# First feed-forward column of a transformer layer: copy, weight halves, sums and the scaling of the last rows emitted in another order

## The chip, the cores and the metric

The kernel runs on one core of one Trainium2 chip. The metric is the device time of one execution in microseconds, as the median of several runs. The engines are named as in the profile: PE (matmul), DVE (vector), ACT (scalar), POOL (GpSimd) and SP, which issues most of the transfers. Each engine works through its own queue in order, and waits on semaphores for the others.

## The reference

One layer of an encoder runs over two sequences of 1024 tokens with model width 1024: attention with low-rank queries and keys, and a Fourier mixing beside it, then a gated feed-forward block, all in float32. The part that matters here is the end of the layer:

```python
    x = x + ga1 * mix
    h2 = rmsnorm(x, g_ffn) * (1.0 + sc2) + sh2
    ffn = (jax.nn.silu(h2 @ w_gate) * (h2 @ w_up)) @ w_down
    return x + ga2 * ffn
```

`w_gate` and `w_up` are 1024 x 2816; the kernel cuts the 2816 into 22 columns of 128.

## The kernel before

**Precision.** A float32 product is made from two halves of each operand: a high half rounded by ACT (L62, a cast) and a low half, the difference, by DVE (L63). `split` and `hl` make them. One product of 128 x 128 x 512 takes three matmuls (L78, L79, L80).

**Seven products instead of eight.** Gate and up weights of a column are a 2 x 2 block matrix, as are the activations (two halves of the width, two halves of the tokens). Four subtractions (`sums_w`) turn a column's four weight blocks into seven operands; the activations have seven as well, `H[0]` to `H[6]`, each with a high tile and a low tile (`H40`, `H41` for operand 4). A column is seven steps in the order of operands 0, 5, 1, 6, 4, 3, 2, and a step is 12 matmuls into one of three PSUM banks x, y, z: x in steps one and three, y in steps two, four and six, z in steps five and seven. Between them ACT copies x (L1358), applies silu (L1367, L1378), and DVE adds banks to values in SBUF (L138) and multiplies (L1379, L1382). A step that goes on in a bank must wait until the sum of that bank has been read.

**Where the stretch lies.** The output projection of the last 256 rows of sequence 1 (`out_proj`, tile `gb`) runs into the first column of sequence 0 (`n` = 0, here column one). At that time four things are unfinished:

- the operands `H[4]`, `H[3]`, `H[2]` of sequence 0, which the generator `prep` loads and splits;
- the weights of column one, of which `sums_w` has made the operands in `w0`; the first two are split before the column (tiles `fw`), the other five inside it (tiles `wh`, `wl`);
- the weights of column two, loaded by SP into four `val` tiles (L1244), summed on DVE (L135) and split;
- the last two blocks of 128 rows (`norm3`). Block `u` = 1 lies in the upper half of tile `X1`. POOL stores these rows to memory (L1149), ACT takes the sum of squares (L1153), POOL makes the reciprocal root (L103 to L110, tile `rs_r`), and DVE scales the rows in place (L1155). In column two `flip2` transposes them (L1162) and ACT and SP write them out as activations of sequence 1.

Besides, POOL makes sums of the down weights (`down_combos`, tile `tdb`, loaded at L1266, stored to `t_d`) and of the weights from column three on (tile `rgu`, loaded at L1248). `rgu` of column three lies in tile `X0`, which first holds `w0`, then the loaded operand 2.

**What sets the order.** A scheduler orders each engine's queue at build time, from the order in which the code emits the instructions. `tc.issue_after(i)` places the instructions emitted under it behind instruction `i`; `behind()` does so for the last high and low half; `first(early, late)` puts one before another.

Of the kernel before, what the change touches and what calls it, by code (L numbers as in the profile page):

```python
# [16 lines left out]
ALU = mybir.AluOpType  # L17
# [35 lines left out]
def hybrid_encoder_kernel(ctx: ExitStack, tc: tile.TileContext, a: dict):  # L53
    nc = tc.nc

    here = {}
# [1017 lines left out]
    with ExitStack() as st:  # L1074
# [72 lines left out]
        def norm3(u, jk=None):  # L1147
            x2 = S.pop(("x2", 1, 3, u))
            nc.gpsimd.dma_start(x2_d[1][(6 + u) * P : (7 + u) * P, :], x2)  # L1149
# [5 lines left out]
            nc.vector.tensor_scalar(out=S["xn", 1, 3, u], in0=x2, scalar1=r[:, 0:1], scalar2=None, op0=ALU.mult)  # L1155

        def flip2(b, xn, bankf, hts):
            for g in range(4):
# [79 lines left out]
        for s in range(2):  # L1238
# [70 lines left out]
            if s == 0:  # L1309
                wts = [(fw[0][:, i, :], fw[1][:, i, :]) for i in range(2)]  # L1310
                fw = None
                next(prep, None)
                wts += [hl(w0[i]) for i in (2, 3)]
            else:
                wts = first_w
            A = {}
            late = None
            for n, f in enumerate(order):
                cur, nxt = wts, []
                src = combos(n + 1, s == 0 and n == 0) if n + 1 < NF else None  # L1320
                if late is not None:
                    put_s(*late)
                    late = None
                elif s == 0 and n > 0:
                    down_combos(n // 2)
                    if n % 4 == 1 and n < 20:
                        comb_h(1, n // 4 - 1) if n >= 5 else None

                def step(j, ps, k, first, src=src):
                    prod(ps, k, cur[j], first)  # L1330
                    if s == 0 and n == 0:
                        if j == 0:
                            cur.extend(hl(v) for v in w0[4:])
                            w0.clear()
                            norm3(1, S.pop("jk3").bitcast(BF16))
                        if j < 3:
                            with behind():
                                for _ in range(2):
                                    next(prep, None)
                            return  # L1340
                        if j == 3:
                            src = S["w1"] = sums_w(src, lambda i: val(), nc.vector)
                        src = S["w1"]
                        for i in ((), (), (), (0, 1), (2, 3), (4,), (5, 6))[j]:
                            nxt.append(hl(src[i]))
                    elif src is not None:
                        with ExitStack() as after:
                            if j == 1:
                                after.enter_context(tc.issue_after(here["p1"]))
                            nxt.append(hl(src[j]))  # L1350
                    if s == 0 and n == 1 and j == 2:
                        S.pop("w1", None)
                        flip2(3, [S.pop(("xn", 1, 3, u)) for u in range(2)], bank, lambda g: val())

                x, y, z = bank(), bank(), bank()
                step(0, x, 0, True)
                p1 = val()
                here["p1"] = nc.scalar.copy(p1, x).ins  # L1358
                step(1, y, 5, True)
                u2 = val()  # L1360
                here["u"] = add(u2, y, p1, nc.vector)
                if pending:
                    with tc.issue_after(here["u"]):
                        pending.pop(0)()
                step(2, x, 1, False)
                sg = val()
                nc.scalar.activation(sg, x, AF.Silu)  # L1367
                step(3, y, 6, False)
                u3 = val()
                here["u"] = add(u3, y, p1, nc.vector)  # L1370
                if pending:
                    with tc.issue_after(here["u"]):
                        pending.pop(0)()
                step(4, z, 4, True)
                add(u3, z, u3, nc.vector)
                step(5, y, 3, False)
                add(p1, y, p1, nc.vector)
                nc.scalar.activation(p1, p1, AF.Silu)  # L1378
                nc.vector.tensor_tensor(out=u3, in0=p1, in1=u3, op=ALU.mult)  # L1379
                step(6, z, 2, False)  # L1380
                add(u2, z, u2, nc.vector)
                nc.vector.tensor_tensor(out=u2, in0=sg, in1=u2, op=ALU.mult)  # L1382
                A[0, n % 2] = u2
# [294 lines left out]
```

## Time and profile before

| | |
|---|---|
| median of 3 runs | 2070.72 us (2069.9 to 2070.88) |
| profiled execution, its own time | 2073.43 us |
| its span, first to last instruction | 2071.7 us |
| PE busy | 2001.2 us, 97% |
| DVE, ACT, POOL busy | 1417.9, 902.8, 831.7 us |
| granted TensorE clock, mean | 0.991 |

In a timeline row stand start, duration, engine, line, operation, the tile written and the tiles read, the shape, and in brackets how long the engine had stood idle before it and what ended that. A matmul's duration overlaps the next one's: the distance of starts is what one costs. In a row of the waits stand the total in us, the times and the longest; in a row of the table by stretches the window, its length, the busy time and count of PE, the weight loads, DVE, ACT and POOL, then the granted clock, the share of the transfer engines and their GB/s.

### The profile page before, as it was taken

To read this page: it belongs to the slowest core of one execution; us is meant where nothing else is said; L and a number is where in the kernel's file an instruction comes from. 1 tells how busy PE (TensorE), PEld (TensorE's weight loads), DVE (VectorE), ACT (ScalarE), POOL (GpSimd) and SP (SyncE) were. 2 spreads that over 40 slices of the span, in tenths; PEclk is the share of its full clock that TensorE was granted. 3 is DMA by queue.
4 is the path that set the end of the run, shared out by engine and by line. 5 is a ranking of instruction groups with operands and counts; after the bars stand their busy time and mean duration, and the time that the engine had idled before them with its cause. 6 is when DMAs were issued, how large, how long until landed. Compare 5 with 4: busy or idle time off the path is not lost.

```text
span 2071.7 us, 28756 instructions
## 1 busy us (share of the span) xinstructions
PE 2001.2 (97%) x10044; PEld 1661.8 (80%) x10044; DVE 1417.9 (68%) x2097; ACT 902.8 (44%) x1765; POOL 831.7 (40%) x1026
## 2 busy tenths in 40 slices
PE   5899999999999997999999999999999999999997
PEld 2788877888888886888888888877788888888876
DVE  2757757766776777887777677777765566567684
ACT  2665534555565564333333356454333333336441
POOL 1455203111312313798788710223554454420142
PEclk8999999999999999999999999999999999999999
DMA  9586775544643465555555578675332232258662
GB/s 367 192 250 207 229 262 191 133 94 90 158 119 116 153 219 178 173 197 189 188 192 178 177 257 271 220 240 178 128 127 101 78 127 102 80 186 278 225 229 91
DMA packets 182942, 371.30 MB, mean 179 GB/s; under 512 B 19020, under 2 KB 58316, under 8 KB 179724
## 3 DMA queue, kind: packets, MB, share of 16 engines
q1 hardware_dynamic: 163660, 309.80, 45.0%
q0 software_dynamic: 19136, 59.65, 9.6%
q8 instruction: 79, 1.29, 0.3%
q14 instruction: 67, 0.55, 0.1%
HBM read 257.38 MB, written 120.39 MB: 182 GB/s over the span
## 4 chain that ended last, share of the span: by engine, by line
PE 52%; DVE 4%; DMA 2%; issue 1%; POOL 1%; ACT 1%; SPq 0%; DVEq 0%; ACTq 0%; POOLq 0%
PE bank L79 18%; PE bank L78 18%; PE bank L80 17%; DVE wl L63 2%; DVE val L138 1%; DMA val<-x_d 1%; DMA draw<-s_d 1%; POOL val L138 1%; DMA draw<-t_d 1%; ACT wh L62 0%; DVE val L1485 0%; POOL rs_y L106 0%; DMA draw<-in_w_down_dram 0%; DVE val L1459 0%; SPq L1444 0%
## 5 line engine op out<-in xcount | busy, mean ns | idle before, releaser
L79 PE MATMUL bank<-H,wh 128*128 128x512 f32 x1224 | 477.4, 390 | 9.3 <-DVE H L63 9.3
L78 PE MATMUL bank<-H,wh 128*128 128x512 f32 x1224 | 477.9, 390 | 5.5 <-DVE val L138 4.1
L80 PE MATMUL bank<-H,wl 128*128 128x512 f32 x1224 | 476.8, 390 | 0.0
L138 DVE TENSOR_TENSOR val<-bank,val 128x512 f32<-128x512 f32 x244 | 166.7, 688 | 166.8 <-PE bank L80 162.6
L79 PEld LDWEIGHTS bank<-H,wh 128*128 128x128 f32 x1224 | 230.3, 188 | 57.2 <-DVE H L63 9.6
L78 PEld LDWEIGHTS bank<-H,wh 128*128 128x128 f32 x1224 | 230.3, 188 | 56.2 <-DVE val L138 6.8
L80 PEld LDWEIGHTS bank<-H,wl 128*128 128x128 f32 x1224 | 230.2, 188 | 48.3
L63 DVE TENSOR_TENSOR wl<-draw,wh 128x512 fp32r<-128x512 f32 x286 | 201.0, 737 | 88.5 <-ACT wh L62 87.2
L62 ACT CAST wh<-draw 128x512 fp32r<-128x512 f32 x286 | 168.6, 620 | 157.3 <-PE bank L79 80.6
L79 PE MATMUL bank<-wl,wh 128*128 128x512 f32 x572 | 223.8, 391 | 2.5 <-DVE wl L63 2.4
L138 POOL TENSOR_TENSOR val<-val 128x512 f32<-128x512 f32 x58 | 83.3, 1444 | 351.0 <-DVE val L1459 186.4
L78 PE MATMUL bank<-wh 128*128 128x512 f32 x572 | 222.7, 389 | 0.0
L80 PE MATMUL bank<-wh,wl 128*128 128x512 f32 x572 | 222.7, 389 | 0.0
L62 ACT CAST wh<-rgu 128x512 fp32r<-128x512 f32 x171 | 106.3, 622 | 248.8 <-PE bank L79 192.8
L63 DVE TENSOR_TENSOR wl<-val,wh 128x512 fp32r<-128x512 f32 x133 | 143.3, 1079 | 74.0 <-ACT wh L62 73.9
L63 DVE TENSOR_TENSOR wl<-rgu,wh 128x512 fp32r<-128x512 f32 x171 | 163.8, 958 | 2.5 <-ACT wh L62 2.4
L62 ACT CAST wh<-val 128x512 fp32r<-128x512 f32 x133 | 82.3, 622 | 183.9 <-PE bank L79 162.5
L135 POOL TENSOR_TENSOR val<-rgu 128x512 f32<-128x512 f32 x80 | 112.6, 1407 | 103.6 <-DMA rgu<-in_wgu_dram 99.9
L79 PEld LDWEIGHTS bank<-wl,wh 128*128 128x128 f32 x572 | 107.3, 188 | 28.9 <-DVE wl L63 6.7
L78 PEld LDWEIGHTS bank<-wh 128*128 128x128 f32 x572 | 107.4, 188 | 22.8 <-ACT wh L62 0.4
L80 PEld LDWEIGHTS bank<-wh,wl 128*128 128x128 f32 x572 | 107.4, 188 | 21.9
L945 DVE TENSOR_REDUCE mx<-ps_s 128x1 f32<-128x1024 f32 x64 | 78.2, 1222 | 60.9 <-PE ps_s L940 60.5
(374 smaller groups left out, 4125.2 us busy)
## 6 DMA issues: line engine op xcount, KB each, us to landing
rgu<-in_wgu_dram SPq DMA_DIRECT2D x86, 512.0 KB
draw<-s_d SPq DMA_DIRECT2D x143, 256.0 KB
s_d<-val POOLq DMA_DIRECT2D x88, 256.0 KB, 4.0
draw<-t_d SPq DMA_DIRECT2D x88, 256.0 KB
s_d<-val SPq DMA_DIRECT2D x66, 256.0 KB
draw<-in_w_down_dram SPq DMA_DIRECT2D x55, 256.0 KB
wada<-in_w_ada_dram SPq DMA_DIRECT2D x13, 1024.0 KB
xt<-in_x_dram SPq DMA_DIRECT2D x16, 512.0 KB
```

What stands on the lines that cost most here:

```text
L62: here["a"] = nc.scalar.copy(hi, src).ins
L63: here["v"] = nc.vector.tensor_tensor(out=lo, in0=src, in1=rd(hi), op=ALU.subtract).ins
L78: nc.tensor.matmul(out, lh, rh, start=first, stop=False, skip_group_check=cont)
L79: nc.tensor.matmul(out, lh, rl, start=False, stop=False, skip_group_check=cont)
L80: nc.tensor.matmul(out, ll, rh, start=False, stop=last, skip_group_check=cont)
L135: return eng.tensor_tensor(out=out, in0=x, in1=y, op=ALU.subtract).ins
L138: return eng.tensor_tensor(out=out, in0=x, in1=y, op=ALU.add).ins
L945: nc.vector.tensor_reduce(out=mx, in_=ps, axis=AX.X, op=ALU.max)
```

## The change

In column one (`opening` in the new code) the preparing work is no longer emitted inside `step`, behind the matmuls, but in a new function `then`, called behind the copy, sum or silu that follows a step:

- after the copy of bank x: the other five weights of column one are split (`w0[2]` first, then 3, 5, 6, 4), and `norm3(1)` is called, which now keeps its scaling back;
- after steps two, three and four: two pieces of `prep` each, that is one of the operands 4, 3, 2, and after step four the kept scaling;
- after step five: the sums of column two's weights;
- after step seven: the first two of these are split. The other five are split in column two, one a step, beside the seven of column three.

```diff
@@ norm3
-            nc.vector.tensor_scalar(out=S["xn", 1, 3, u], in0=x2, scalar1=r[:, 0:1], scalar2=None, op0=ALU.mult)
+            xn = S["xn", 1, 3, u]
+
+            def scale():
+                nc.vector.tensor_scalar(out=xn, in0=x2, scalar1=r[:, 0:1], scalar2=None, op0=ALU.mult)
+
+            if u == 0:
+                scale()
+            else:
+                S["scale"] = scale
@@ before the columns
-                wts += [hl(w0[i]) for i in (2, 3)]
@@ step
+                opening = s == 0 and n == 0
                 def step(j, ps, k, first, src=src):
                     prod(ps, k, cur[j], first)
-                    if s == 0 and n == 0:
-                        if j == 0:
-                            cur.extend(hl(v) for v in w0[4:])
...
-                        if j < 3:
-                            with behind():
-                                for _ in range(2):
-                                    next(prep, None)
-                            return
-                        if j == 3:
-                            src = S["w1"] = sums_w(src, lambda i: val(), nc.vector)
-                        src = S["w1"]
-                        for i in ((), (), (), (0, 1), (2, 3), (4,), (5, 6))[j]:
-                            nxt.append(hl(src[i]))
...
+                    if opening or src is None:
+                        return
+                    if s == 0 and n == 1 and j + 2 < 7:
+                        cur.append(hl(S["w1"][j + 2]))
...
+                def then(j, src=src):
...
+                    if j == 0:
+                        with tc.issue_after(here["p1"]):
+                            got = {2: hl(w0[2])}
+                            S["wl2"] = here["v"]
+                            got.update((i, hl(w0[i])) for i in (3, 5, 6, 4))
+                            cur.extend(got[i] for i in range(2, 7))
                             w0.clear()
                             norm3(1, S.pop("jk3").bitcast(BF16))
+                    elif j < 4:
+                        if j == 1:
+                            first(S.pop("wl2"), here["u"])
+                        with tc.issue_after(here["u"]), behind():
+                            for _ in range(2):
+                                next(prep, None)
+                            if j == 3:
+                                S.pop("scale")()
+                    elif j == 4:
+                        with tc.issue_after(here["v"]):
+                            S["w1"] = sums_w(src, lambda i: val(), nc.vector)
+                    elif j == 6:
+                        nxt.extend(hl(v) for v in S["w1"][:2])
```

Each engine issues as many instructions as before; only their order differs, from the head of column one to the end of column two. Three places show it.

DVE before, behind the last sum of the projection (`X1<-X1,gb`). The second row is the scaling, the five `wl` rows are low halves of column one's weights, `H41` and `H31` are the low halves of operands 4 and 3:

```order
L878 TENSOR_TENSOR X1_8622<-X1_8622,gb_8779 128x512
L1155 TENSOR_SCALAR X1_8622<-X1_8622,rs_r_8855 128x1024
L63 TENSOR_TENSOR wl_8807<-rgu0_8619,wh_8804 128x512
L63 TENSOR_TENSOR wl_8811<-H41_8635,wh_8810 128x512
L63 TENSOR_TENSOR wl_8838<-rgu0_8619,wh_8837 128x512
L63 TENSOR_TENSOR wl_8842<-H41_8635,wh_8841 128x512
L63 TENSOR_TENSOR wl_8846<-rgu0_8619,wh_8845 128x512
L63 TENSOR_TENSOR H41_8864<-H20_8642,H40_8863 128x1024 x2
L138 TENSOR_TENSOR val_8892<-bank_8823,val_8872 128x512
L63 TENSOR_TENSOR H31_8887<-H21_8655,H30_8886 128x1024 x2
```

The same place now:

```order
L878 TENSOR_TENSOR X1_8622<-X1_8622,gb_8779 128x512
L63 TENSOR_TENSOR wl_8832<-rgu0_8619,wh_8829 128x512
L63 TENSOR_TENSOR wl_8836<-H41_8635,wh_8835 128x512
L63 TENSOR_TENSOR wl_8840<-H41_8635,wh_8839 128x512
L63 TENSOR_TENSOR wl_8844<-rgu0_8619,wh_8843 128x512
L63 TENSOR_TENSOR wl_8848<-rgu0_8619,wh_8847 128x512
L138 TENSOR_TENSOR val_8876<-bank_8813,val_8827 128x512
L63 TENSOR_TENSOR H41_8879<-H20_8642,H40_8878 128x1024 x2
L63 TENSOR_TENSOR H31_8902<-H21_8655,H30_8901 128x1024 x2
L138 TENSOR_TENSOR val_8919<-bank_8813,val_8827 128x512
L63 TENSOR_TENSOR H21_8922<-X0_8884,H20_8921 128x1024 x2
L1158 TENSOR_SCALAR X1_8622<-X1_8622,rs_r_8857 128x1024
```

The scaling has gone behind the weights, two sums out of banks (`val<-bank`, u2 and u3) and the operands 4, 3 and 2.

DVE now, right behind that scaling: sums out of banks, the subtractions for column two (L135) and the low halves of column two's weights (`wl_8978`, `wl_8982`, `wl_9026`, `wl_9048`; `wl_9030` is of column three):

```order
L138 TENSOR_TENSOR val_8919<-bank_8814,val_8919 128x512
L135 TENSOR_TENSOR val_8941<-val_8807,val_8806 128x512
L138 TENSOR_TENSOR val_8827<-bank_8813,val_8827 128x512
L135 TENSOR_TENSOR val_8806<-val_8806,val_8804 128x512
L63 TENSOR_TENSOR wl_8978<-val_8804,wh_8977 128x512
L135 TENSOR_TENSOR val_8942<-val_8807,val_8806 128x512
L1404 TENSOR_TENSOR val_8919<-val_8827,val_8919 128x512
L135 TENSOR_TENSOR val_8943<-val_8805,val_8942 128x512
L138 TENSOR_TENSOR val_8876<-bank_8814,val_8876 128x512
L63 TENSOR_TENSOR wl_8982<-val_8942,wh_8981 128x512
L1407 TENSOR_TENSOR val_8876<-val_8899,val_8876 128x512
L63 TENSOR_TENSOR wl_9026<-val_8805,wh_9025 128x512
```

Before, the four subtractions stood around the second half of operand 2, and all seven low halves of column two stood ahead of column one's last sum.

POOL now, behind the store of the last rows; `rs_v` to `rs_r` make the reciprocal root for the scaling, `tdb` is of the down weights:

```order
L1149 DMA x2_d1_103<-X1_8622 128x1024
L135 TENSOR_TENSOR tdb_8995<-tdb_8995 128x512
L103 TENSOR_SCALAR rs_v_8854<-ms2_8852 128x1
L106 TENSOR_TENSOR rs_y_8855<-rs_v_8854,mhalf_70 128x1
L1283 DMA t_d_106<-tdb_8995 128x512
L107 TENSOR_TENSOR rs_w_8856<-rs_y_8855 128x1
L108 TENSOR_TENSOR rs_w_8856<-rs_w_8856,rs_v_8854 128x1
L109 TENSOR_SCALAR rs_w_8856<-rs_w_8856 128x1
L110 TENSOR_TENSOR rs_r_8857<-rs_w_8856,rs_y_8855 128x1
```

Before, the six operations of the reciprocal root came first and the `tdb` operation and its store behind them. On SP the load of `g_final` (tile `gf`) now stands before the two loads of operand 2 into `X0`, and behind them nothing moves until column two.

More of the change, by code (lines that the diff above doesn't have):

```diff
@@ L1327, in hybrid_encoder_kernel @@
                         comb_h(1, n // 4 - 1) if n >= 5 else None
+                opening = s == 0 and n == 0
                 def step(j, ps, k, first, src=src):
                     prod(ps, k, cur[j], first)
[L1331 to L1333 removed]
+                    if opening or src is None:
+                        return
+                    if s == 0 and n == 1 and j + 2 < 7:
+                        cur.append(hl(S["w1"][j + 2]))
+                    with ExitStack() as after:
+                        if j == 1:
+                            after.enter_context(tc.issue_after(here["p1"]))
+                        nxt.append(hl(src[j]))
+                    if s == 0 and n == 1 and j == 4:
+                        S.pop("w1")
+                    if s == 0 and n == 1 and j == 2:
+                        flip2(3, [S.pop(("xn", 1, 3, u)) for u in range(2)], bank, lambda g: val())
@@ new lines, in then @@
+                def then(j, src=src):
+                    if not opening:
+                        if pending and j in (1, 3):
+                            with tc.issue_after(here["u"]):
+                                pending.pop(0)()
+                        return
+                    if j == 0:
[4 more added lines that the diff above has]
+                            cur.extend(got[i] for i in range(2, 7))
@@ L1351, in step @@
-                    if s == 0 and n == 1 and j == 2:
-                        S.pop("w1", None)
-                        flip2(3, [S.pop(("xn", 1, 3, u)) for u in range(2)], bank, lambda g: val())
+                    elif j < 4:
+                        if j == 1:
+                            first(S.pop("wl2"), here["u"])
[9 more added lines that the diff above has]
+                        nxt.extend(hl(v) for v in S["w1"][:2])
```

17 lines of the change are left out of this document (6 added, 11 removed).

## The prediction

> **What bounds the kernel now.** I read the page first, then the PE timeline around the first feed-forward column, then the DVE, ACT, POOL and SP timelines of the same stretch, and last the waits of PE after it. The page's first part, and the header row of its chain:
>
> ```profile
> PE 2001.2 (97%) x10044; PEld 1661.8 (80%) x10044; DVE 1417.9 (68%) x2097; ACT 902.8 (44%) x1765; POOL 831.7 (40%) x1026
> PE 52%; DVE 4%; DMA 2%; issue 1%; POOL 1%; ACT 1%; SPq 0%; DVEq 0%; ACTq 0%; POOLq 0%
> ```
>
> PE is busy 97% of the span, so an edit pays only where PE stands still or runs slowly. The PE timeline shows such a place in column one (columns one and two are `n` = 0 and 1 of sequence 0):
>
> ```profile
> 777.04 0.39 PE L78 MATMUL bank<-H,fw 128*128 128x512 f32 x1
> ...
> 781.57 0.39 PE L80 MATMUL bank<-H,fw 128*128 128x512 f32 x1
> ...
> 782.25 0.39 PE L80 MATMUL bank<-H,fw 128*128 128x512 f32 x1
> 784.11 0.49 PE L78 MATMUL bank<-H,wh 128*128 128x512 f32 x1 [1.47 <-ACT H L62]
> 793.90 0.80 PE L79 MATMUL bank<-H,wh 128*128 128x512 f32 x1 [9.29 <-DVE H L63]
> 794.49 0.63 PE L78 MATMUL bank<-H,wh 128*128 128x512 f32 x1
> ...
> 798.33 0.43 PE L78 MATMUL bank<-H,wh 128*128 128x512 f32 x1
> ...
> 817.66 1.91 PE L1162 MATMUL bank<-ident,X 128*128 128x128 f32 x16
> 820.22 0.50 PE L78 MATMUL bank<-H,wh 128*128 128x512 f32 x1 [0.65 <-DVE val L138]
> ...
> 831.27 0.39 PE L78 MATMUL bank<-H,wh 128*128 128x512 f32 x1
> ```
>
> Column one starts at 777.04, column three at 831.27: 54.23 us. Three matmuls start in 0.68 (781.57 to 782.25), 0.2267 each; the 168 of two columns are 38.1 us, and the 16 transposes about 1.95. So 14.2 us are lost: 1.63 before 784.11, 9.56 before 793.90, 2.2 from there to 798.33 and 0.8 around 820.22. The 2.2 is the clock, in the table by stretches (PEclk is the third number from the end):
>
> ```profile
> 784.60:788.20 3.60, 0.01 (x1) 0.00 (x0) 0.32 (x1) 3.30 (x5) 0.14 (x1) 0.99 0.42 170
> 788.20:793.90 5.70, 0.00 (x1) 0.00 (x1) 5.70 (x8) 0.00 (x0) 2.21 (x2) 0.50 0.15 51
> 793.90:798.20 4.30, 4.30 (x10) 3.47 (x11) 4.30 (x5) 1.04 (x1) 0.00 (x0) 0.50 0.98 345
> ```
>
> The grant falls to 0.50 after 3.6 us of standstill and stays there for 4.3 us of work; the 1.6 us before 784.11 cost no clock. Who was late is in the DVE timeline:
>
> ```profile
> 787.88 0.75 DVE L1155 TENSOR_SCALAR X<-X,rs_r 128x1024 f32<-128x1024 f32 x1 [8.59 <-DMA x_d<-X]
> 788.55 1.75 DVE L63 TENSOR_TENSOR wl<-rgu,wh 128x512 fp32r<-128x512 f32 x1
> 790.22 0.68 DVE L63 TENSOR_TENSOR wl<-H,wh 128x512 fp32r<-128x512 f32 x1
> 790.83 0.68 DVE L63 TENSOR_TENSOR wl<-rgu,wh 128x512 fp32r<-128x512 f32 x1
> ...
> 792.63 2.35 DVE L63 TENSOR_TENSOR H<-H,H 128x1024 fp32r<-128x1024 f32 x2
> 794.90 0.68 DVE L138 TENSOR_TENSOR val<-bank,val 128x512 f32<-128x512 f32 x1
> ```
>
> The scaling of the last 128 rows writes over memory that POOL's store still reads, and waits 8.59 us for it; the five low halves of weights and operand 4 stand behind it on DVE, and PE waits for operand 4. What bounds the stage is this one queue position. The rest of the path carries any gain to the end: the longest waits of PE from 820 to the end are
>
> ```profile
> PE bank L78 <- DVE val L138: 4.1, 5, 1.1
> PE bank L79 <- DVE wl L63: 2.4, 5, 0.9
> ```
>
> and behind column two every engine keeps its order.
>
> **The change, part by part.** The rows for ACT, POOL and SP:
>
> ```profile
> 780.43 0.60 ACT L62 CAST wh<-rgu 128x512 fp32r<-128x512 f32 x1
> 782.50 0.61 ACT L62 CAST wh<-rgu 128x512 fp32r<-128x512 f32 x1
> 783.02 1.99 ACT L62 CAST H<-H 128x1024 fp32r<-128x1024 f32 x2
> 784.91 0.57 ACT L1358 COPY val<-bank 128x512 f32<-128x512 f32 x1
> 796.57 1.04 ACT L62 CAST H<-X 128x1024 fp32r<-128x1024 f32 x1 [8.67 <-DMA X<-hc_d]
> 779.59 0.65 POOL L1149 DMA_DIRECT2D x_d<-X  x1 [2.82 <-DVE X L878]
> 780.94 0.57 POOL L106 TENSOR_TENSOR rs_y<-rs_v,mhalf 128x1 f32<-128x1 f32 x1
> 788.05 1.70 POOL L135 TENSOR_TENSOR tdb<-tdb 128x512 f32<-128x512 f32 x1 [5.46 <-DMA tdb<-in_w_down_dram]
> 806.89 1.27 POOL L135 TENSOR_TENSOR val<-rgu 128x512 f32<-128x512 f32 x1 [16.19 <-DMA rgu<-in_wgu_dram]
> 779.46 0.38 SPq L1266 DMA_DIRECT2D tdb<-in_w_down_dram  x1
> 792.73 0.89 SPq L1100 DMA_DIRECT2D X<-hc_d  x2
> 802.08 0.83 SPq L1248 DMA_DIRECT2D rgu<-in_wgu_dram  x2
> ```
>
> Copy and weights. The copy of the first bank moves from 784.91 to the head of ACT's queue, 779.95 (end of the first 12 matmuls) to 780.5, where the square of the last rows stood; the five casts stay at 780.4 to 783.1. DVE no longer waits: the five low halves follow the casts, the first ready at 781.7, the fifth at 784.2. PE ends step two of the column at 777.04 + 24 x 0.2267 = 782.5 and has what it needs; the gap of 1.63 and that of 9.56 go, and the clock's 2.2 with them.
>
> Operand 4: ACT takes the moved square (about 1.2 with its read-out) and the two casts (1.99) to 786.2, DVE's two halves (2.35) end at 787.6; PE wants them at 782.48 + 5.44 = 787.9. Price nothing, cover 0.3.
>
> Operand 3: silu, two casts to 788.7, DVE to about 790.0. POOL's op on tdb at 788.05 lies beside it; the row at 788.55 took 1.75 beside that same op where 0.68 is usual, so add 1.07: 791.1. Then u3's add, 0.68, which reads the bank that step six writes: 791.7. PE wants 790.64: **1.05 lost**.
>
> Operand 2: its load waits for the fifth low half, so issue at 784.2 instead of 792.73. The row shows 3.8 us to the first half's use; the queue is fuller now (tdb, X's store, and gf's load, which is moved ahead of it and issues about 782.7), so I take 5 to 6, 790, the second half 1.3 later. ACT ends at 792.4, DVE at 791.7 + 2.35 = 794.05. PE ends step six at 791.7 + 2.72 = 794.4, does two early matmuls of column two, and starts step seven at 794.9: nothing lost, cover 0.8.
>
> The scaling now stands behind operand 2 on DVE, behind the op on tdb on POOL. tdb at 788.05 + 1.70, then rs_v, the power (0.57), a DMA issue (0.65) and four small ops of about 0.27: 792.9. The store is down at 787.9 as now. DVE is free at 794.05, so the scaling waits for nothing; its 0.67 of queue is paid below. Its readers, the transposes, come after 805.
>
> Sums on DVE, an operand a step. Behind the scaling stand two adds and two subtractions (0.6 each) and the first low half of column two: 794.75 + 2.4 + 0.68 = 797.85. PE ends step seven at 797.6: **0.25 lost**. Ten matmuls to 800.1, two more to 800.55; the next low half is five rows on. Here POOL enters: the load of column three's weights issues when operand 2 is split, 794.1 instead of 802.08, and with the 4.8 us to POOL's first op on it that is 798.9. From then POOL runs without a pause, as it did from 806.89. What DVE's ops took beside it then, count and mean:
>
> ```profile
> L63 DVE TENSOR_TENSOR wl<-val,wh 128x512 fp32r<-128x512 f32 x4 | 7.0, 1767 | 0.0
> L138 DVE TENSOR_TENSOR val<-bank,val 128x512 f32<-128x512 f32 x4 | 2.7, 679 | 0.0
> L63 DVE TENSOR_TENSOR wl<-rgu,wh 128x512 fp32r<-128x512 f32 x2 | 1.9, 925 | 0.0
> L1379 DVE TENSOR_TENSOR val<-val 128x512 f32<-128x512 f32 x1 | 1.8, 1776 | 0.0
> L1382 DVE TENSOR_TENSOR val<-val 128x512 f32<-128x512 f32 x1 | 1.8, 1771 | 0.0
> ```
>
> Ops with both inputs outside PSUM: 12.5 us in 8, 1.56 each; the adds out of a bank stay at 0.68. So from 799.0: a subtraction to 800.6, an add to 801.2, the low half to 802.75. **2.2 lost**; bounds are 0.3 (0.6 each, as without POOL) and 7 (the rival below). Then step two ends at 805.0, eleven transposes 806.3; DVE is at 805.9 with the third weight and at 809.6 with the fourth and the add before it, PE wants the latter at 809.65. From there DVE gains on PE. ACT's high halves for them wait in line behind one that needs POOL's third op (798.9 + 4.7 = 803.6), and the first of them is due at 812: cover 8. The later tdb load and its op on POOL go behind the loads and ops of column four's weights; only stores for the down projection follow from them: nothing. So the five splits moved into column two cost nothing further, by a cover of 0.05 to 0.4: it is gone as soon as DVE's mean is above 1.56.
>
> The Trainium skill, "SBUF — State Buffer", section "SBUF: two separate sides", says that the port pair of DVE and GpSimd is an exclusive lock and that whoever comes second blocks for the whole instruction. The row at 788.55 agrees: it ended 0.55 after POOL's op. An estimate by that rule for strict turns with POOL's 1.27 is about 1.9 an op; the sum would lose about 2 us more.
>
> The sum: 1.05 + 0.25 + 2.2 = 3.5 lost where 14.2 were; gain 10.7. Column three starts at 820.6, the span is 2061.0, the profiled execution's own time 2062.7 instead of 2073.43. That one lay 2.7 above the median of the runs, 2070.72, so the forecast is **2060.0**.
>
> **The rivals.** First, *DVE bounds column two*: each of six DVE ops from 799.0 waits out a whole POOL op. The group of four above averages 1.77 with single ops up to
>
> ```profile
> 817.13 2.43 DVE L63 TENSOR_TENSOR wl<-val,wh 128x512 fp32r<-128x512 f32 x1
> ```
>
> At 2.43 each the six cost 5.2 more, less 0.4 of cover: gain 5.9, 2064.8. For it: twelve splits now lie in column two where there were seven. Against: the group of two averages 0.93 in the same stretch. The lock quoted from the skill's SBUF page would be its mechanism.
>
> Second, *POOL pauses*: DVE's ops run at 0.68 throughout, the 1.05 and the 2.2 vanish: gain about 14, 2056.7. Against: both rows above.
>
> Third, *operand 2 is the new wait*: gf and tdb ahead of its load delay it to where it lands now, 796.5. ACT and DVE then need 3.5 more, step seven starts at 800 instead of 794.9, and with a gap of 5 the clock takes about 1.5: gain 4, 2066.7. For it: gf's 512 KB are put in front. Against: the DMA share is 0.42 from 784.6 to 788.2 and 0.15 after.
>
> Fourth, slower: *tdb's load holds the scaling*. If it lands at T, the reciprocal root comes at T + 4.85, and scaling to first low half of column two take 3.75: PE waits for T + 8.6. At 788.05 that is 796.65, 1.2 under what I have. A wait of 8.5 with its clock loss cancels the gain, T = 797.8, 18 us after the issue against 8.6 now; at T = 802 the time is 2074.9. For it: two loads more behind it in the same engines; against: it stands ahead of them in SP's queue.
>
> That the change does not do what it says is excluded by the order shown above: the scaling stands thirteen operations later.
>
> **How the numbers follow.** Forecast 0.60, DVE-bound 0.16, POOL pauses 0.10, operand 2 late 0.09 (a third of it still above the bound), slower 0.05. About 0.2%, 4.1 us, is what a measurement of this kernel can tell from no change: faster 0.60 + 0.16 + 0.10 + 0.03 = 0.89, same 0.06, slower 0.05. The range takes in the second and the first rival, 2056.5 to 2065.2, and leaves out the last two, 0.14.
>
> **What would show it.** Right: no DVE wait for the store of X, the copy at 780, PE's clock at 1.00 throughout, PE gaps of about 1 before step six and 2 before the second product of column two, column three at 820 to 822. Wrong: a PE gap over 3.6 us anywhere between 782 and 821, an X load landing after 794, or DVE ops in column two averaging 2 us or more.

## The result, and the profile after

The changed kernel takes **2063.9 us** (median of 8 runs, 2061.74 to 2065.44) where the kernel before took 2069.86 (8 runs, 2068.31 to 2070.88) beside it: a ratio of 0.997, interval 0.9959 to 0.9981. That is 6.0 us, three in a thousand; the forecast was 2060.0, with a range of 2056.5 to 2065.2. The profiled execution took 2064.13, its span 2062.4.

The page's first part and the header row of its chain show nearly the same busy times as before in a shorter span:

```profile
PE 2000.4 (97%) x10044; PEld 1661.1 (81%) x10044; DVE 1421.2 (69%) x2097; ACT 903.3 (44%) x1765; POOL 838.8 (41%) x1026
PE 54%; DVE 2%; DMA 1%; POOL 1%; issue 1%; ACT 1%; SPq 0%; DVEq 0%; POOLq 0%; ACTq 0%
```

The table by stretches, cut at the starts of column one, column two and column three, first of before, then of after (PEclk is the third number from the end):

```profile
777.04:809.49 32.45, 21.69 (x85) 17.25 (x84) 23.15 (x28) 14.43 (x22) 7.08 (x11) 0.84 0.52 177
809.49:831.27 21.78, 21.13 (x101) 17.50 (x100) 16.44 (x18) 10.23 (x19) 11.73 (x11) 1.00 0.53 183
831.27:2071.00 1239.73, 1223.70 (x5377) 1007.40 (x5375) 865.62 (x1055) 465.02 (x821) 594.75 (x586) 1.00 0.52 175
```

```profile
778.33:801.25 22.92, 20.16 (x85) 15.46 (x84) 18.28 (x23) 11.86 (x17) 7.63 (x9) 1.00 0.66 225
801.25:823.52 22.27, 21.73 (x101) 17.29 (x100) 21.70 (x23) 12.63 (x24) 15.53 (x12) 1.00 0.57 192
823.52:2062.00 1238.48, 1223.13 (x5377) 1007.70 (x5375) 869.25 (x1056) 465.03 (x821) 596.48 (x587) 1.00 0.51 176
```

Column one went from 32.45 to 22.92 at a clock of 1.00, column two from 21.78 to 22.27: the two together from 54.23 to 45.19 us. At 0.2267 a matmul and 1.95 for the transposes they could take 40.0, so 5.2 are still lost. PE's timeline has most of them (its rows with a wait, and the first rows of column one, at 778.33, and of column three, at 823.52); the rest lies in starts further apart than 0.2267, most of them beside these waits:

```profile
778.33 0.39 PE L78 MATMUL bank<-H,fw 128*128 128x512 f32 x1
...
784.45 0.50 PE L78 MATMUL bank<-H,wh 128*128 128x512 f32 x1 [0.53 <-ACT wh L62]
...
789.37 0.47 PE L78 MATMUL bank<-H,wh 128*128 128x512 f32 x1 [1.62 <-DVE val L138]
...
798.85 0.50 PE L78 MATMUL bank<-H,wh 128*128 128x512 f32 x1 [0.61 <-DVE val L138]
...
804.77 0.50 PE L80 MATMUL bank<-H,wl 128*128 128x512 f32 x1 [0.19 <-DVE wl L63]
...
812.17 0.50 PE L78 MATMUL bank<-H,wh 128*128 128x512 f32 x1 [0.33 <-DVE val L138]
...
823.52 0.39 PE L78 MATMUL bank<-H,wh 128*128 128x512 f32 x1
```

The wait of 9.29 is gone, and in its place stand five short ones, 3.3 in all. The first two, 0.53 and 1.62, share a cause, which ACT's, DVE's and POOL's timelines name:

```profile
781.25 0.59 ACT L1384 COPY val<-bank 128x512 f32<-128x512 f32 x1 [3.20 <-PE bank L80]
783.78 0.62 ACT L62 CAST wh<-rgu 128x512 fp32r<-128x512 f32 x1 [1.95 <-PE bank L79]
```

```profile
784.43 0.69 DVE L63 TENSOR_TENSOR wl<-rgu,wh 128x512 fp32r<-128x512 f32 x1 [3.83 <-ACT wh L62]
786.25 2.38 DVE L63 TENSOR_TENSOR wl<-rgu,wh 128x512 fp32r<-128x512 f32 x2
788.55 0.68 DVE L138 TENSOR_TENSOR val<-bank,val 128x512 f32<-128x512 f32 x1
...
797.45 0.75 DVE L1158 TENSOR_SCALAR X<-X,rs_r 128x1024 f32<-128x1024 f32 x1
798.11 0.69 DVE L138 TENSOR_TENSOR val<-bank,val 128x512 f32<-128x512 f32 x1
```

```profile
786.38 1.69 POOL L135 TENSOR_TENSOR tdb<-tdb 128x512 f32<-128x512 f32 x1 [4.83 <-DMA tdb<-in_w_down_dram]
```

The copy comes where it was forecast, 2.9 us into the column, but the first cast behind it waits 1.95 us more for a matmul of PE, one that has nothing to do with the weight being cast. PE's second step reads `fw`, the weights split before the column. In the changed code `val` tiles (the first are those of column two's weights) are allocated ahead of the first `wh` tile. The reading is that this `wh` tile now lies in memory that `fw` had, so that the cast may write only when the last matmul on `fw` has read; kernel 3 below tests it. The casts began 5.5 us into the column where 3.4 was forecast, and the fifth low half ended 10.3 into it instead of 7.2. The last two low halves took 2.38 for the pair, as POOL's operation on `tdb` lay beside them. u2's add behind them (788.55) held step four by 1.62. The scaling at 797.45, on the other hand, waits for nothing.

### The profile page after: what moved, and what is told of

Read it like the earlier page. It is cut to its first block, busy times and chain, and to the rows that moved or that the text cites. A ratio compares the mean times of both kernels' runs of the same rounds, so it can differ in the third digit from the quotient of the medians.

```text
span 2062.4 us, 28756 instructions
## 1 busy us (share of the span) xinstructions
PE 2000.4 (97%) x10044; PEld 1661.1 (81%) x10044; DVE 1421.2 (69%) x2097; ACT 903.3 (44%) x1765; POOL 838.8 (41%) x1026
## 3 DMA queue, kind: packets, MB, share of 16 engines
q8 instruction: 79, 1.29, 0.3%
## 4 chain that ended last, share of the span: by engine, by line
PE 54%; DVE 2%; DMA 1%; POOL 1%; issue 1%; ACT 1%; SPq 0%; DVEq 0%; POOLq 0%; ACTq 0%
PE bank L79 18%; PE bank L78 18%; PE bank L80 18%; DVE wl L63 1%; DVE val L138 1%; POOL val L138 1%; DMA val<-x_d 1%; DMA draw<-t_d 1%; ACT wh L62 0%; DVE val L1511 0%; POOL rs_y L106 0%; DMA draw<-s_d 0%; DVE val L1500 0%; DVE val L1404 0%; POOL rs_v L105 0%
## 5 line engine op out<-in xcount | busy, mean ns | idle before, releaser
L135 POOL TENSOR_TENSOR val<-rgu 128x512 f32<-128x512 f32 x80 | 112.7, 1408 | 95.1 <-DMA rgu<-in_wgu_dram 86.2
```

The source lines that it names most:

```text
L135: return eng.tensor_tensor(out=out, in0=x, in1=y, op=ALU.subtract).ins
```

## The experiments

They were timed in three further sets of runs, each beside the kernel before (2072.52, 2072.42 and 2072.84 there). What is compared first is what every profile gives: the start of column one, the two columns (84 matmuls each, counted in PE's order, from the start of the first to that of the next column's), and the rest behind them.

| kernel | start | column one | column two | both | rest | time, median | ratio (interval) |
|---|---|---|---|---|---|---|---|
| before | 777.04 | 32.45 | 21.78 | 54.23 | 1240.4 | 2069.86 | |
| before, again | 776.97 | 31.20 | 20.84 | 52.04 | 1240.0 | 2072.42 (15 runs) | |
| after | 778.33 | 22.92 | 22.27 | 45.19 | 1238.9 | 2063.90 | 0.997 (0.9959 to 0.9981) |
| after, again | 775.07 | 22.88 | 22.26 | 45.14 | 1239.7 | 2064.40 | 0.9962 (0.9948 to 0.9976) |
| 1 scaling alone | 776.36 | 24.70 | 22.52 | 47.22 | 1241.2 | 2065.43 | 0.9967 (0.9954 to 0.998) |
| 2 all but the scaling | 778.38 | 26.35 | 30.55 | 56.90 | 1240.2 | 2071.37 | 0.9996 (0.9984 to 1.0009) |
| 3 early `wh` | 775.82 | 21.03 | 22.52 | 43.55 | 1239.7 | 2063.26 | 0.9952 (0.9941 to 0.9964) |
| 3, again | 779.52 | 23.25 | 22.28 | 45.53 | 1238.4 | 2063.56 | 0.9951 (0.9938 to 0.9965) |
| 4 all seven in column one | 777.72 | 22.81 | 29.01 | 51.82 | 1239.1 | 2070.63 | 0.999 (0.9981 to 0.9998) |
| 5 DVE's order sharpened | 776.68 | 21.58 | 25.56 | 47.14 | 1241.6 | 2067.17 | 0.9975 (0.9966 to 0.9984) |
| 6 POOL's sums left out | 774.62 | 25.23 | 20.84 | 46.07 | 1239.7 | 2062.17, one run | |
| 7 `tdb` later | 778.26 | 21.28 | 25.55 | 46.83 | 1240.1 | 2064.43 | 0.9959 (0.9946 to 0.9971) |

**1 and 2: which part brings the gain.** The first kernel is the one before with only the scaling moved, behind operand 3 on DVE; the copy, the weights and the sums stay.

```diff
@@ norm3: as in the change, scale() kept back for u == 1
@@ step, j < 3 of column one
                             for _ in range(2):
                                 next(prep, None)
+                                if j == 2:
+                                    S.pop("scale")()
```

> The kernel before with one edit: the scaling of the last 128 rows is kept back until behind the operands 4 and 3 (now after H31 on DVE); weights, sums, copy and memory stay as before. Theory A (the stall was only the scaling's place in DVE's queue): the 9.3 us wait of PE and its clock loss go, a gap of about 1.6 before operand 4 and one of about 1 behind it stay; column one to column three takes 43 to 46 us instead of 54.2, and the time is 6 to 10 us under the kernel before, that is as good as the changed kernel or better. Rival B (the gain comes from the new order of copy, weights and sums; the scaling is one wait among several): under 3 us gained.

The second is the changed kernel without that part: the scaling falls where the scheduler puts it, between the halves of operand 4.

```diff
-            if u == 0:
-                scale()
-            else:
-                S["scale"] = scale
+            scale()
...
-                            if j == 3:
-                                S.pop("scale")()
```

> The changed kernel with the scaling no longer kept back: it then stands between the two halves of operand 4 on DVE and waits for the store of its rows and for the reciprocal root, which now stands behind tdb on POOL. Theory A: DVE stops there until about 793, operand 4 is 4 to 6 us late for PE, the time is 3 to 6 us above the changed kernel. Rival B: within 1.5 us of the changed kernel.

Moving the scaling alone took the two columns from 54.23 to 47.22, 7.0 us, and the median 7.1 (2072.52 before). The median is inside theory A's 6 to 10; the columns missed its 43 to 46, as PE still waits 1.45, 1.61 and, in column two, 1.43. Everything else without it gave 56.90, no gain, and a median of 2071.37, 1.2 under before with an interval that takes in no change; it is 7 over the changed kernel of the next set, where theory A had 3 to 6. In DVE's timeline the scaling waits for POOL's root, and a sum out of a bank that PE hasn't finished stands ahead of the subtractions:

```profile
791.32 0.75 DVE L1158 TENSOR_SCALAR X<-X,rs_r 128x1024 f32<-128x1024 f32 x1 [0.91 <-POOL rs_r L110]
...
802.44 0.69 DVE L138 TENSOR_TENSOR val<-bank,val 128x512 f32<-128x512 f32 x1 [2.77 <-PE bank L80]
```

PE then waits three times, 2.65, 3.67 and 2.37 us, and its clock falls (0.65 in the 4.2 us behind the first wait). Not all of this is the scaling's doing. The first of these waits ended with a cast that stood on ACT behind the second half of operand 2, and that half's load came late:

```profile
796.17 1.04 ACT L62 CAST H<-X 128x1024 fp32r<-128x1024 f32 x1 [1.87 <-DMA X<-hc_d]
```

Kernel 2's twelve runs also spread from 2064.66 to 2077.24, and the profiled one took 2077.24, 5.9 above their median. What is shown is that the place of the scaling in DVE's queue is the gain: moved alone, it gains as much by the median, 7.1, as the whole change (6.0 and 8.0 in its two sets). The columns are 2 shorter in the changed kernel's profile (47.22 to 45.19), but a gain in time from the order of the rest is not resolved, with the scaling moved or without.

**3: the missed wait.** The changed kernel, with the first `wh`, `gf`, `tdb` and `wl` tiles allocated ahead of the `val` tiles, so that `wh` doesn't lie on `fw`; each engine's order stays the same.

```diff
                 next(prep, None)
+                w5.tile([P, 512], F32R, tag="wh", name="wh", bufs=8)
+                S["gf"] = w5.tile([P, D], F32, name="gf")
+                w5.tile([P, 2, 512], F32, tag="ga", name="tdb", bufs=1)
+                w5.tile([P, 512], F32R, tag="wl", name="wl", bufs=8)
```

> The changed kernel with the tiles wh, gf, tdb and wl given their memory before the first val tile, as in the kernel before; the order of all instructions stays. In the changed kernel the first cast of column one's weights waits for the last matmul that reads fw, because wh lies where fw lay: 3.3 us later than forecast. Theory A (that wait makes up most of what is missing of the forecast gain): casts start at 1.5 us after the copy instead of 2.5 to 3.5 later, the PE gaps of 0.5 and 1.6 before steps three and four go or shrink to under 1 in sum, 1.5 to 2.5 us under the changed kernel. Rival C (what is missing is DVE's blocking by POOL in column two): within 0.7 us of the changed kernel.

In its ACT timeline the cast follows the copy at once:

```profile
778.74 0.59 ACT L1388 COPY val<-bank 128x512 f32<-128x512 f32 x1 [3.22 <-PE bank L80]
779.22 0.62 ACT L62 CAST wh<-rgu 128x512 fp32r<-128x512 f32 x1
```

The waits of 0.53 and 1.62 before steps three and four become 0 and 0.39. So the wait hung on where the tile lies, as read above. The columns take 43.55 where the forecast had 43.5. The second profile of the same kernel had been expected at 43.5 again, within 0.3, and gave 45.53: there operand 2's load, issued at 787.52, came late, and ACT waited for it.

```profile
795.48 1.05 ACT L62 CAST H<-X 128x1024 fp32r<-128x1024 f32 x1 [4.53 <-DMA X<-hc_d]
```

The same transfer took 8.0 us from issue to first use here and 4.6 in the first profile. Against before of its own set this kernel is a little further down than the changed one (ratios 0.9952 and 0.9951 beside 0.997 and 0.9962), but the intervals overlap: the wait is shown gone, a gain in time is not resolved.

**4: the five splits.** The changed kernel, with all seven operands of column two split at the end of column one instead of two there and five in column two.

```diff
-                    if s == 0 and n == 1 and j + 2 < 7:
-                        cur.append(hl(S["w1"][j + 2]))
...
-                        nxt.extend(hl(v) for v in S["w1"][:2])
+                        nxt.extend(hl(v) for v in S.pop("w1"))
```

> The changed kernel with all seven weights of column two split at the end of column one, instead of two there and five in column two. By the forecast (cover of 0.05 to 0.4 us in column two, nothing gained or lost by the split itself): within 1.5 us of the changed kernel. Rival C (twelve splits in column two make DVE the bound there): 1.5 to 4 us under the changed kernel.

All theories had it within a few us of the changed kernel or under it, and all were wrong: 6.6 us more in the columns, 6.2 by the medians (2070.63 and, in the next set, 2064.40). DVE's timeline:

```profile
805.58 9.24 DVE L63 TENSOR_TENSOR wl<-val,wh 128x512 fp32r<-128x512 f32 x5
814.74 0.68 DVE L63 TENSOR_TENSOR wl<-rgu,wh 128x512 fp32r<-128x512 f32 x1
815.34 0.68 DVE L138 TENSOR_TENSOR val<-bank,val 128x512 f32<-128x512 f32 x1
```

Five low halves in a row, 1.85 each beside POOL, stand ahead of the add that frees the bank, and PE waits 4.99 for it. Spreading the five over column two is what keeps that add in time.

**5: the order sharpened further.** Kernel 3, with u2's add behind the second low half instead of the fifth, the scaling behind an add that PE waits for, and the first two splits of column two directly behind their subtractions. With it the square of the last rows went ahead of the copy on ACT, and the reciprocal root ahead of the `tdb` operation on POOL.

```diff
                     if j == 0:
-                            got = {2: hl(w0[2])}
-                            S["wl2"] = here["v"]
-                            got.update((i, hl(w0[i])) for i in (3, 5, 6, 4))
+                            cur.append(hl(w0[2]))
+                            cur.append(hl(w0[3]))
+                            S["wl2"] = here["v"]
...
                         if j == 1:
                             first(S.pop("wl2"), here["u"])
+                            with tc.issue_after(here["u"]):
+                                got = {i: hl(w0[i]) for i in (5, 6, 4)}
...
                     elif j == 4:
                         with tc.issue_after(here["v"]):
+                            S.pop("scale")()
                             S["w1"] = sums_w(src, lambda i: val(), nc.vector)
+                            nxt.extend(hl(v) for v in S["w1"][:2])
```

> The kernel with the early wh tiles, in which DVE's queue is ordered further: in column one the add for u2 stands behind the low half that step four needs instead of behind all five, the scaling behind the add for u3 that step seven waits for, and the second low half of column two ahead of the multiplication and of the fourth subtraction. That kernel's PE waits were 0.39 before step four, 0.48 before step seven and 0.39 before the second product of column two. Theory A (DVE's order is what is left): these three go, with the slow matmul starts around them 1.3 to 2.0 us in all, stretch 41.7 to 42.3 instead of 43.55, ratio 0.994 to 0.9955. Rival C (DVE is at its limit beside POOL): the waits only move on to the low halves of column two behind, stretch 43 to 43.6, same time as the kernel with the early tiles.

Slower than kernel 3 by 3.6 in the columns (by 1.6 beside its second profile), which neither theory had. The first four steps run at 2.72 each, without a wait; then PE waits for DVE after all, 1.19 before step six and 0.85 before step seven, and in column two something new happens. POOL's timeline, then ACT's:

```profile
800.86 4.06 POOL L135 TENSOR_TENSOR val<-rgu 128x512 f32<-128x512 f32 x1 [11.24 <-DMA rgu<-in_wgu_dram]
```

```profile
807.69 1.14 ACT L62 CAST wh<-val 128x512 fp32r<-128x512 f32 x2 [5.92 <-POOL val L135]
```

POOL's first operation takes 4.06; its next three take 1.28 to 1.30. DVE ran five operations out of SBUF back to back from 800.68 to 803.77, each at 0.68, and POOL's ended 1.15 after the last of them, as if it had waited them out. Casts of column two stand in ACT's queue behind one that needs POOL's sums, DVE's low halves behind the casts, and PE waits 2.80 at 816.67. So the faster DVE of one stretch seems to have made the late DVE of the next.

**6: POOL beside DVE.** The changed kernel with eight operations of POOL left out.

```diff
+                if s == 0 and n == 2:
+                    for _ in range(3):
+                        val()
+                    return [b11, b21, b21, b12, b12, b22, b22]
...
-                sub(b11, b12, b11, nc.gpsimd)
+                if f:
+                    sub(b11, b12, b11, nc.gpsimd)
...
```

> The changed kernel with POOL's elementwise work beside columns one and two left out: the four subtractions for column three's weights and the four of the first down weights are not computed, their inputs are used in their places, so that only the root's small operations and the transfers' issues are left on POOL. Theory C (DVE's long operations come from POOL working beside it): the low halves and the multiplication in column two take 0.68 instead of 1.77, the pair of low halves before u2's add 1.29 instead of 2.38, PE waits in column two for nothing (1.3 us less from column two to column three, 21.0 instead of 22.27), and step four of column one begins 1.1 earlier. Theory A agrees on the operations; by it the wait of 1.95 of the first cast for the last matmul that reads fw stays, so stretch about 42.5 to 43 instead of 45.19. If DVE's long operations have another cause (their operands, the transfers) they stay at 1.77 and the stretch at 45.

The groups of DVE from 801 to 812 in the changed kernel, and the same window here (count, busy time in us, mean in ns):

```profile
L63 DVE TENSOR_TENSOR wl<-val,wh 128x512 fp32r<-128x512 f32 x4 | 5.4, 1360 | 0.0
L1407 DVE TENSOR_TENSOR val<-val 128x512 f32<-128x512 f32 x1 | 1.8, 1775 | 0.0
L63 DVE TENSOR_TENSOR wl<-rgu,wh 128x512 fp32r<-128x512 f32 x1 | 1.8, 1774 | 0.0
```

```profile
L63 DVE TENSOR_TENSOR wl<-val,wh 128x512 fp32r<-128x512 f32 x6 | 4.1, 684 | 0.1
L63 DVE TENSOR_TENSOR wl<-rgu,wh 128x512 fp32r<-128x512 f32 x4 | 2.7, 682 | 0.0
L1416 DVE TENSOR_TENSOR val<-val 128x512 f32<-128x512 f32 x1 | 0.7, 687 | 0.0
```

With POOL still, every operation takes 0.68, and column two 20.84 instead of 22.27. So POOL is the cause of DVE's long operations, and they cost column two 1.4 us. In column one, u2's add came 1.1 earlier (9.1 into the column instead of 10.2). But the column grew, and the two columns missed the 42.5 to 43: operand 2's second half came late, ACT waited 2.55 for it, and step seven took 5.99. Without its sums POOL sent two stores at about the time of that load (782.83 and 784.21, the loads from 783.86); that they delayed it was not tested. The total is no measure of POOL's price, column two is.

**7: POOL's first operation later.** Kernel 3, with the operation on `tdb` behind the sums for column three.

```diff
-                    down_combos(n // 2)
+                    with ExitStack() as after:
+                        if n == 1:
+                            after.enter_context(tc.issue_after(here["s"]))
+                        down_combos(n // 2)
```

> The kernel with the early wh tiles, in which POOL's first operation on the down weights (tdb) and its store stand behind the four subtractions for column three's weights instead of ahead of the reciprocal root; nothing else moves. In that kernel the four low halves of operands 4 and 3 took 5.46 beside POOL (4.68 at 1.17 each would be free of it), and PE waited 0.24 before step six and 0.48 before step seven. Theory A (the price of POOL's work beside DVE is paid where it lies, and column two has cover at its end): those two waits shrink by about 0.8 in all, column one 20.2 instead of 21.03, column two as it was, stretch 42.5 to 43.0 instead of 43.55. Rival C (DVE pays wherever POOL works): column two grows by 0.5 or more, as one POOL operation of 1.7 more lies beside its low halves, and the stretch stays at 43.3 to 44. By either the time is within 1.5 of the kernel with the early tiles.

The four low halves of operands 4 and 3 took 4.62 instead of 5.46, as expected. But POOL's next operation again took long beside a run of five DVE operations, 4.10 us, and column two took 25.55: more than rival C had, in the manner of kernel 5. By the median it is 0.9 over kernel 3 of the same set, inside the 1.5; the profiled execution lay 2.6 above that median. What could separate the kernels is which DVE operation runs when POOL's first arrives. In the changed kernel a sum out of a bank follows soon:

```profile
802.92 0.69 DVE L138 TENSOR_TENSOR val<-bank,val 128x512 f32<-128x512 f32 x1
803.52 1.20 DVE L63 TENSOR_TENSOR wl<-val,wh 128x512 fp32r<-128x512 f32 x1
804.64 1.77 DVE L1407 TENSOR_TENSOR val<-val 128x512 f32<-128x512 f32 x1
```

```profile
802.19 1.98 POOL L135 TENSOR_TENSOR val<-rgu 128x512 f32<-128x512 f32 x1 [8.38 <-DMA rgu<-in_wgu_dram]
804.25 1.62 POOL L135 TENSOR_TENSOR rgu<-rgu 128x512 f32<-128x512 f32 x1
```

POOL's operation ends 1.25 after that sum begins, about the 1.27 that it takes alone, and from then the two engines take turns, 1.77 and 1.62. In kernels 5 and 7 the next such sum began 3.1 and 3.3 us after POOL's operation had begun. The profiles of kernels 1, 3 and 4 fit (a bank sum within 0.4 us of POOL's first operation, which takes 1.28 to 1.60). In kernel 2 and in the second profile of before, however, POOL got in between two of DVE's operations out of SBUF (803.19 and 805.87, 1.68 long each), having begun 0.15 after one of them; in kernel 7 it began 0.12 after one and was held. So a bank sum goes with POOL getting in, but what decides it is open; no run changed it alone.

**The same kernels again.** 

> The changed kernel itself, once more, on the chip of this set of runs. Open is why the columns one and two gave 9.0 us in its profile (54.23 to 45.19 from the start of column one to that of column three) and the medians only 6.0. Theory A (the gain is that stretch and nothing else, and the kernel before varies from run to run by the length of its standstill): stretch 45.2 +- 0.3 again, the median 6 to 9 us under the kernel before of these runs, 2 to 4 us over the kernel with the early wh tiles (ratio 0.9952). Rival D (something behind column two gives part of the gain back): the stretch is as short, and the rest of the span is 2 us or more longer than in the kernel before.

> The kernel before, once more, for a second profile of its standstill. Theory A: the store of the last rows takes 6 to 10 us, the scaling waits for it to its end, and the stretch of columns one and two differs from 54.23 by as much as the time differs from that of the first profile (2073.4), within 1 us. Rival D: the wait is the same within 0.3 us, and the time differs elsewhere.

In before's second profile the scaling waited 7.62 for the store instead of 8.59 (786.85), PE 8.32 instead of 9.29, and the columns took 52.04 instead of 54.23: the span is 2.7 shorter, 2.2 of it here. 1.2 of that is column one, where the scaling's wait for the store ended 1.0 sooner, and 0.9 column two, so not all of it is the standstill. The changed kernel repeats its two columns within 0.05 us; its distance to kernel 3, 0.8 to 1.1 by the medians, is under the 2 to 4 of theory A. From column three on every profile has 1238.4 to 1241.6, so nothing is given back later: rival D falls. The median gained 8.0 in that set, where the columns of its two profiles differ by 6.9; in the first set the two were 6.0 and 9.0. A gain read from one pair of profiles agrees with that of the medians only within 3 us here.

## Why the prediction was right, and where its steps failed

**The bound** was right. One place in DVE's queue held PE; kernel 1 moves it alone and gets 7.0 of the 9.0 us. The clock is 1.00 in both columns, as forecast, the copy comes in time, and the scaling waits for nothing (797.45; forecast 794.05). Of the other signs that were named, the gaps of 1 before step six and 2 before the second product did not come, column three began at 823.52 instead of 820 to 822 (column one began 1.3 later), and one sign of being wrong did come, an X load that lands after 794 (below). The median, 2063.9, lies 3.9 above the forecast and 1.3 under the upper bound, and that bound was set by the first rival, which didn't come; that the range held it is in part luck.

**"The five casts stay at 780.4 to 783.1"** failed: they ran from 783.78. The step counted with ACT's queue and the copy, and not with where the tile that they write lies. An edit that changes the order in which tiles are allocated moved them to other memory here, with a wait that no data flow shows. The price: steps two, three and four took 3.40, 4.92 and 2.81 for 2.72 each, 3.0 lost where none was forecast; with the tile elsewhere they lose 0.7.

**Operands 4 and 3.** Operand 4 cost nothing, as said. For operand 3 1.05 was forecast, for POOL's operation on `tdb` beside DVE; 0 came there, as PE itself was 3.0 late. The slowing was as large as said (a pair of low halves in 2.38, 1.29 in kernel 6), but it fell on the last two weights, ahead of u2's add, and so is 1.1 of the 3.0: without it, in kernel 6, steps two, three and four lose 1.9. Where PE is in time (kernel 3), steps five and six lose 0.5.

**Operand 2: "nothing lost", use at 790.** The loads issued with the fifth low half, from 788.65, and the first use came 4.0 later, sooner than the 5 to 6 taken. The second half was the late one, 2.6 behind the first use where 1.3 was taken: ACT waited 1.52 for its load, and DVE 0.81 for ACT.

```profile
795.23 1.05 ACT L62 CAST H<-X 128x1024 fp32r<-128x1024 f32 x1 [1.52 <-DMA X<-hc_d]
796.30 1.23 DVE L63 TENSOR_TENSOR H<-X,H 128x1024 fp32r<-128x1024 f32 x1 [0.81 <-ACT H L62]
```

Step seven lost 0.9 where nothing was forecast: the add that frees its bank (798.11) stands behind this half and the scaling, and PE waited 0.61 for it. The third rival, a late operand 2, is there in small; in kernel 3's second profile it cost most of 2 us. The 1.5 that this rival gave to the clock behind a gap of 5 was too little: in kernel 4, behind a wait of 4.99, the clock stood at 0.50 until 821, and the next 12 matmuls took 5.29 instead of 2.72.

**Sums and POOL in column two.** 0.25 was forecast at the head of column two, and 2.2 before its second product. 0 and 0.5 came, and 0.8 more behind, where nothing was forecast (1.3 in all, 22.27 less 20.99). The price of an operation was higher than taken, 1.77 against 1.56. But POOL, whose first operation began at 802.19, held DVE up only from the bank sum at 802.92 on; the two subtractions and the multiplication ahead of the second low half, of which one was priced at 1.56, took 0.6 each. The Trainium skill, "SBUF — State Buffer", section "SBUF: two separate sides", has the port pair that DVE and GpSimd share as a lock held for a whole instruction; the prediction's estimate by it, 1.9 an operation, was nearer than the 1.56 of the row. The first rival's 2.43 each didn't come, the second rival (DVE at 0.68 throughout) came only where POOL's work was left out.

**"The five splits moved into column two cost nothing further"** held only while DVE's mean stayed at 1.56, a condition that the prediction named. At 1.77 PE waited 0.33 for an add behind three low halves (812.17). The step also missed what the move is for: left in column one the five cost 6.6 (kernel 4).

**The sum** was 3.5 lost, and 5.2 were: 43.5 forecast for the columns, 45.19 measured. In steps two to four 3.0 came for 0, before step six 0 for 1.05, in step seven 0.9 for 0, in column two 1.3 for 2.45. Kernel 3, without the missed wait, had 43.55 in its first profile, but that it meets the forecast is luck: its four terms are 0.7, 0.5, 0.8 and 1.5, and its second profile gave 45.53.

**From the profile to the median.** The gain of the profiled execution, 10.7, was taken for that of the medians. The two profiled executions differ by 9.3 (2073.43 and 2064.13), the medians by 6.0 with an interval of 3.9 to 8.5, because the profiled execution of before lay 3.6 above the median of its eight runs. What the columns took in those other runs is not on record. Before's second profile shows that they vary, by 2.2; against it the changed kernel gains 6.9 there. The start of column one wanders as well, from 774.6 to 779.5 among the twelve profiles, though the change begins only there; why stays open.

## What to carry to other kernels

An instruction that waits for a transfer costs what stands behind it in its queue: move the one instruction first, and ask of everything else in the edit what it is worth alone. When an edit moves an allocation, look up which tile's memory each new tile takes over and when that one is last read. On two engines that shut each other out, the order on one can decide when the other gets in: with a queue packed without a break, two profiles lost more behind the second engine than they saved on the first (kernels 5 and 7).

## What the runs showed that was not expected

POOL's operations on 128x512 in SBUF and DVE's with two SBUF inputs excluded each other, in two manners: in turns (1.62 and 1.77 against 1.27 and 0.68 alone), or with POOL held off through a whole run of DVE (4.06 and 4.10 for one operation). By the Trainium skill, "SBUF — State Buffer", section "SBUF: two separate sides", the later one blocks for the whole instruction of the other; these rows show that it can be five in a row. DVE's sums out of a PSUM bank stayed at 0.67 to 0.69 in every one of these stretches. POOL's tiny operations became longer as well: in the changed kernel three of the root's steps on 128x1 took 1.05 each beside DVE's halves, where the same steps took 0.19 while DVE stood still:

```profile
777.62 0.19 POOL L109 TENSOR_SCALAR rs_w<-rs_w 128x1 f32<-128x1 f32 x1
...
791.63 1.05 POOL L109 TENSOR_SCALAR rs_w<-rs_w 128x1 f32<-128x1 f32 x1
```
